# Attention of a two-layer hybrid block on one core: values of three key tiles in one line, newest first, and the last layer's probability sums by products of ones

## Chip, cores and metric

One core of a Trainium2 chip runs the whole program. The metric is the time of one execution on the device in microseconds (us); lower is better. Three executions of the kernel before were timed; a fourth one was taken with the hardware profiler, and every duration below is from that one.

## What is computed

Two layers; each normalises 512 latent and 256 context tokens of width 1024, projects them, runs three token mixers side by side (a recurrent one, a latent attention with 8 heads over all keys, and a grouped attention with 8 heads, a window of 128 and a sink), gates and merges their outputs, and projects back. The change touches the two attentions alone:

```python
def dense_block_attention(q, k, v):
    ...
        s = jnp.einsum('bqhd,bkhd->bhqk', qx, k, preferred_element_type=jnp.float32) * (Dq ** -0.5)
        p = jax.nn.softmax(s, axis=-1).astype(v.dtype)
        return jnp.einsum('bhqk,bkhd->bqhd', p, v)
...
def sink_gqa(q, k, v, sink, valid):
    ...
    s = jnp.where(valid, s, NEG)
    sk = jnp.broadcast_to(sink.astype(jnp.float32).reshape(C_KV_HEADS, C_GROUP, 1, 1), s.shape[:-1] + (1,))
    p = jax.nn.softmax(jnp.concatenate([s, sk], axis=-1), axis=-1)[..., :-1].astype(v.dtype)
    return jnp.einsum('bkgqs,bskd->bqkgd', p, v).reshape(B, Q, H * D)
```

In layer 0 both the 512 latent and the 256 context queries are computed, in the last layer the latent ones alone.

## The kernel before, in words

The program is written as one stream of operations with a scheduler behind it: `band` sets the priority of what is written inside it, the scheduler then puts each engine's instructions in an order by readiness (by its own estimate) and priority, and the chip runs each engine's list in that order. The band `SERVE` (line 84) is ahead of all others. `in_line` (line 148) adds, for each product written inside it, that it comes after the product written before it, in PE's order only; nothing else is forbidden to stand between two of them.

**Attention of one head** (`attend`, lines 1103 and 1314). Keys go in tiles of 128; the queries' 512 latent columns (and in layer 0 apart from them 256 context columns) stand side by side. Per key tile the scores `stp` are two or three products into one of three PSUM banks, which the row maxima `mps` of the next head share. ACT makes the exponentials `pe` from them (`probs`, line 879, the ACT instruction at 882), and POOL adds these up in `acc` (886). `prepare` makes the next head's operands and maxima in between (transposes `trp` or `qtp`, maxima `mps`, `mxp`), and `turns` (833) weaves the two.

**Values.** Each tile's (exponentials, values) goes into the list `late`. `together` (854) takes the oldest three when five or more wait and calls `values` for each (1062 and 1247), which calls `weigh` (932): two float32 products per tile, one for each half of the queries, into `yps` (or `ypc` for the context): the output of one half lies in partitions 0 to 63, that of the other in 64 to 127, 64 output columns of the array each, where scores, maxima and projections use 128. In the trace a float32 product is two MATMULs.

**The end of a head.** `normalise` (889) copies the sums of values (`tb`, 894), forms the sums of probabilities over the partitions of `acc`, and multiplies by their reciprocal (925). With `cols` (the last layer) the sums come as columns: four products of `acc`'s 128 columns with one column of ones, and with the sink's (`er`); a reciprocal of 128x4 (907); and products that spread the columns back over 64 partitions (`rec` times the identity). Without `cols` (layer 0) two products of ones with 256 columns give the sums already spread, the sink comes by eight products of 32 rows, and the reciprocal is 128x256 (924). `gate_out` (783) then loads the gate, multiplies (796) and stores to HBM (792).

**What stands around it.** Filler: the rest of the input projections (`g<-hh`, `g<-hl`), which `pace` and `gates` write in a lower band; in the last layer also the merges of the first two mixers, `early` (1371) and `branch` (1343; `g<-yh`, `g<-yl`). Their operands come from HBM (`ygt`, 1351), are rounded by ACT (`yh`, 1352) with the remainder from POOL (`yl`, 1353), and lie where the input projections' operands (`hh`, `hl`) lay before. `tail` (1382) merges the third mixer, which needs the last head's output, and projects back.

Of the kernel before, what the change touches and what calls it, by code (L numbers as in the profile page):

```python
# [19 lines left out]
P = 128  # L20
# [40 lines left out]
def build(tc, A, out):  # L61
# [737 lines left out]
    def gated(*a):  # L799
        gate_out(*a)  # L800
        yield
# [49 lines left out]
            for _ in x:  # L851
                pass

    def together(late, values, rest=False):

        while len(late) >= (1 if rest else EB - 3):
            for _ in range(min(len(late), 3)):
                values(*late.pop(0))

    def max_tile():  # L860
        return rps.tile([P, 512], F32, tag="r", name="mps", bufs=RB)
# [24 lines left out]
            G.tensor_tensor(acc, keep.pop(0, acc), e, ALU.add)  # L886
        return e

    def normalise(ap, yps, acc, n, y, cols, sink=None):

        h, nt = n // 2, n // P
        tb = ap.tile([P, 256], F32, tag="tb", name="tb", bufs=2)[:, 0:h]
        lo, hi = slice(0, 64), slice(64, 128)
        S.copy(tb, yps)
        yield
        if cols:

            sps = rps.tile([P, 256 + nt], F32, tag="c", name="sps", bufs=CB)
            col, sps = sps[:, 256:256 + nt], sps[:, 0:h]
            for t in range(nt):  # L900
                mm(col[:, t:t + 1], acc[:, t * P:(t + 1) * P], ones[:, 0:1], start=(t == 0), stop=(sink is None),
                   skip_group_check=True)
            if sink:
                er, xr, r0 = sink
                mm(col, er, ident[xr, r0:r0 + nt], start=False, skip_group_check=True)
            rec = ap.tile([P, 4], F32, tag="rec", name="rec", bufs=2)[:, 0:nt]
            V.reciprocal(rec, col)
            for t in range(nt // 2):
                for a, u in ((lo, t), (hi, t + nt // 2)):
                    mm(sps[a, t * P:(t + 1) * P], rec[:, u:u + 1].to_broadcast([P, 64]), ident, start=(t == 0),  # L910
                       skip_group_check=True)
            rec = sps
        else:
            sps = rps.tile([P, 256], F32, tag="c", name="sps", bufs=CB)[:, 0:h]
            for a, c0 in ((lo, 0), (hi, h)):
                mm(sps[a], ones[:, 0:64], acc[:, c0:c0 + h], stop=(sink is None), skip_group_check=True)
            if sink:
                er, xr, r0 = sink
                for t in range(nt // 2):
                    for a, u in ((lo, t), (hi, t + nt // 2)):  # L920
                        mm(sps[a, t * P:(t + 1) * P], ident[xr, r0 + u:r0 + u + 1].to_broadcast([er.shape[0], 64]), er, start=False, stop=(t == nt // 2 - 1),
                           skip_group_check=True)
            rec = ap.tile([P, 256], F32, tag="rec", name="rec", bufs=2)[:, 0:h]
            V.reciprocal(rec, sps)
        V.tensor_tensor(y, tb, rec, ALU.mult)

    def value_sums(n):
        if n == 512:
            return gps.tile([P, 512], F32, tag="m", name="yps", bufs=1)[:, 0:n // 2]
        return rps.tile([P, 512], F32, tag="c", name="ypc", bufs=CB)[:, 0:n // 2]  # L930

    def weigh(o, v, e, c0, first, done):


# [117 lines left out]
    def mla_heads(l, last, ap, qt, kt, vh, scale, tq0, filler):  # L1052
# [8 lines left out]

        def values(hd, k, s0, n, e, acc, y):
            nk = 6 if s0 else 2
            if k == 0:
                sums[hd, s0] = value_sums(n)
            weigh(sums[hd, s0], vh[:, k, hd], e, 0, k == 0, k == nk - 1)
            if k == nk - 1:
                later.append(normalise(ap, sums.pop((hd, s0)), acc[:, s0 - qo:s0 + n - qo], n,
                                       y[:, hd % 2, (s0 - qo) // 2:(s0 + n - qo) // 2], last))
                next(later[-1])  # L1070
                if s0 and hd % 2:
                    later.append(gated(ap, l, 4 + hd // 2, y, segs))
# [30 lines left out]
        def attend(hd):  # L1103
            kh, kl, qh, ql = heads[hd]
            par = hd % 2
            if par == 0:
                ys[hd // 2] = ap.tile([P, 2, (T - qo) // 2], F32, tag="y", name="ymla", bufs=2)
            y = ys[hd // 2]
            acc = ap.tile([P, T - qo], F32, tag="acc", name="acc", bufs=2)
            keep = {}  # L1110
            for s0, n, k in [(s0, n, k) for s0, n in segs[::-1] for k in range(6 if s0 else 2)]:
                ks, sl = slice(k * P, (k + 1) * P), slice(s0 - qo, s0 + n - qo)
                st = rps.tile([P, 512], F32, tag="r", name="stp", bufs=RB)[:, 0:n]
                mm(st, kh[0:xr.stop, ks], qh[0:xr.stop, sl], stop=False)
                mm(st, kl[:, ks], qh[0:96, sl], start=False, stop=False)
                mm(st, kh[0:96, ks], ql[:, sl], start=False)
                late.append((hd, k, s0, n, probs(ap, st, n, scale, acc[:, sl], k, keep, EB), acc, y))
                together(late, values)
                if s0:
                    yield  # L1120
            if hd == 7:
                together(late, values, True)

        turns(8, prepare, attend, later, filler)

# [110 lines left out]
    def gqa_heads(l, F, last, ap, KA, KB, vh, sink8, queries, xs, filler):  # L1236
# [9 lines left out]

        def values(hd, k, g0, s0, e, acc, y):
            kv, nk, n = hd // 4, 6 if g0 else 2, (T if g0 else NC) - g0
            if k == 0:
                sums[hd, g0] = value_sums(n)  # L1250
            weigh(sums[hd, g0], vh[:, k, kv], e, s0 - g0, k == 0, k == nk - 1)
            if k == nk - 1:
                later.append(normalise(ap, sums.pop((hd, g0)), acc[:, g0 - qo:g0 + n - qo], n,
                                       y[:, hd % 2, (g0 - qo) // 2:(g0 + n - qo) // 2], last,
                                       (sinks[hd][xr], xr, xr.start - tq0 + g0 // P)))
                next(later[-1])
                if g0 and hd % 2:
                    later.append(gated(ap, l, 8 + hd // 2, y, segs))

        def prepare(hd):  # L1260

# [52 lines left out]
        def attend(hd):  # L1314
# [7 lines left out]
            for g0, n, k in [(g0, n, k) for g0, n in segs[::-1] for k in range(6 if g0 else 2)]:  # L1322
# [8 lines left out]
                    mm(st[:, o_:o_ + P], win[:, 0], win[:, w], start=False, stop=(e == len(edges) - 1),  # L1331
                       skip_group_check=True)
                late.append((hd, k, g0, s0, probs(ap, st, n, scale, acc[:, s0 - qo:s1 - qo], k, keep, EB), acc, y))
                together(late, values)
                if g0:
                    yield
            if hd == 7:
                together(late, values, True)

        turns(8, prepare, attend, later, filler)  # L1340

# [316 lines left out]
```

## Time and profile before

| what | value |
|---|---|
| median of three runs | 2422.4 us (2420.09 to 2424.84) |
| the profiled execution | 2427.43 us, its span 2425.7 us |
| granted TensorE clock, mean | 0.948 |
| busy: PE, PE's loads, DVE, ACT, POOL | 89%, 68%, 52%, 37%, 36% |
| attention of layer 0 | about 780 to 1160 us of the span |
| attention of the last layer | about 2085 to 2290 us |

PE is TensorE's products, PEld its weight loads, DVE VectorE, ACT ScalarE, POOL GpSimd, SPq the queue that issues DMAs. The end of a PE product is modelled and products overlap, so what one costs in its place is read from the starts of neighbours, not from its length. The granted clock is given as a share of 2.4 GHz.

### The profile page before, as it was taken

Reading aid. Unit: us, or ns where it says so; the run is one execution under the profiler, and the core shown is the slowest. Engines: PE = TensorE matmul, PEld = TensorE weight load, DVE = VectorE, ACT = ScalarE, POOL = GpSimd, SP = SyncE. Lnnn points to the kernel's source line nnn. Section 1 sums busy time; section 2 is a strip of 40 time slices with the busy share of each in tenths; the row PEclk is TensorE's granted clock in tenths of the full one; section 3 lists DMA queues with packets and bytes.
Section 4 is the critical chain, followed back from the end, with each engine's and each line's share of the span. In section 5 each row is a group of like instructions: output and inputs, shape, how many; then the busy total and the mean of one; then the engine's idle time right before and its main releaser. Section 6 shows DMA issues by size and latency. Waiting matters only on the chain. (4 is left out here: it accounts for less than half of the span.)

```text
span 2425.7 us, 42832 instructions
## 1 busy us (share of the span) xinstructions
PE 2148.9 (89%) x16824; PEld 1647.0 (68%) x16824; DVE 1271.8 (52%) x2300; ACT 891.7 (37%) x1654; POOL 870.0 (36%) x699
## 2 busy tenths in 40 slices
PE   7986896887998999899888998799868998999989
PEld 4765674766887667766767786567656876666667
DVE  4475326865338664366135256725668457554423
ACT  3443211233354333543213345332323455434322
POOL 1255211111123344444334224553211144454564
PEclk9988998998999999999989999899978999999999
DMA  7155665555251012511686414566444262102385
GB/s 249 60 144 175 194 197 138 138 132 136 74 170 50 31 44 84 189 33 51 205 256 188 134 57 123 163 206 169 121 113 101 86 209 92 48 18 70 106 261 168
DMA packets 330442, 314.25 MB, mean 130 GB/s; under 512 B 112768, under 2 KB 239488, under 8 KB 330240
## 3 DMA queue, kind: packets, MB, share of 16 engines
q1 hardware_dynamic: 312432, 281.87, 39.5%
q10 hardware_dynamic: 17808, 29.63, 3.9%
q8 instruction: 133, 2.18, 0.4%
q14 instruction: 69, 0.57, 0.1%
HBM read 213.64 MB, written 97.78 MB: 128 GB/s over the span
## 5 line engine op out<-in xcount | busy, mean ns | idle before, releaser
L166 POOL TENSOR_TENSOR wl<-wf,wh 128x512 fp32r<-128x512 f32 x316 | 425.7, 1349 | 1064.0 <-ACT wh L165 977.2
L154 PE MATMUL g<-hh,wh 128*128 128x512 f32 (+1 forms) x1264 | 471.3, 373 | 19.2 <-DVE st L779 10.2
L154 PE MATMUL g<-hh,wl 128*128 128x512 f32 (+1 forms) x1264 | 457.0, 362 | 1.5 <-POOL wl L166 1.4
L154 PE MATMUL g<-hl,wh 128*128 128x512 f32 (+1 forms) x1264 | 456.4, 361 | 0.0
L165 ACT CAST wh<-wf 128x512 fp32r<-128x512 f32 x316 | 195.1, 619 | 500.7 <-PE g L154 249.3
L154 PEld LDWEIGHTS g<-hh,wh 128*128 128x128 f32 x1264 | 249.1, 197 | 71.9 <-issue 15.4
L154 PEld LDWEIGHTS g<-hh,wl 128*128 128x128 f32 x1264 | 249.3, 197 | 41.1 <-issue 7.9
L154 PEld LDWEIGHTS g<-hl,wh 128*128 128x128 f32 x1264 | 249.9, 198 | 40.1 <-issue 11.4
L886 POOL TENSOR_TENSOR acc<-acc,pe 128x512 f32<-128x512 f32 (+2 forms) x128 | 146.2, 1142 | 141.2 <-ACT pe L882 131.7
L882 ACT ACTIVATE pe<-stp 128x256 f32<-128x256 f32 (+2 forms) x224 | 114.4, 522 | 201.1 <-PE stp L154 194.4
L864 DVE TENSOR_REDUCE mx<-mps 128x1 f32<-128x384 f32 (+2 forms) x256 | 127.8, 535 | 69.2 <-PE mps L154 67.0
L154 PE MATMUL yps<-pe,vh 128*64 128x256 f32 (+1 forms) x704 | 133.3, 389 | 0.0
L678 DVE TENSOR_TENSOR YB<-YB,inv 128x30 f32<-128x30 f32 (+9 forms) x180 | 96.4, 536 | 5.3
L154 PE MATMUL g<-yh,wh 128*128 128x512 f32 (+1 forms) x224 | 81.4, 368 | 19.9 <-DVE zt L1368 11.4
L1368 DVE SCALAR_TENSOR_TENSOR zt<-zt,g 128x512 f32<-128x512 f32 (+1 forms) x56 | 31.7, 576 | 117.6 <-PE g L154 85.3
L676 DVE TENSOR_TENSOR inv<-inv,YB 128x30 f32<-128x30 f32 (+9 forms) x180 | 87.3, 485 | 8.5 <-issue 2.3
L777 ACT ACTIVATE st<-g 128x256 f32<-128x256 f32 (+1 forms) x108 | 56.6, 524 | 89.1 <-PE g L154 83.7
L154 PE MATMUL g<-yl,wh 128*128 128x512 f32 (+1 forms) x224 | 83.5, 374 | 6.1 <-POOL yl L1353 6.1
L154 PE MATMUL gc<-hh,wh 128*128 128x512 f32 x192 | 76.7, 400 | 8.6 <-ACT hh L325 4.5
L154 PE MATMUL g<-yh,wl 128*128 128x512 f32 (+1 forms) x224 | 80.4, 363 | 0.0
L154 PE MATMUL scps<-AR,BK 64*128 64x128 f32 (+1 forms) x768 | 65.5, 296 | 14.5 <-DVE TR L644 10.6
L154 PE MATMUL gc<-hl,wh 128*128 128x512 f32 x192 | 78.0, 406 | 0.1
(395 smaller groups left out, 4358.2 us busy)
## 6 DMA issues: line engine op xcount, KB each, us to landing
wf<-w_in SPq DMA_DIRECT2D x163, 256.0 KB, 3.1
wf<-ada_w SPq DMA_DIRECT2D x84, 256.0 KB, 4.0
wf<-w_in ACTq DMA_DIRECT2D x77, 256.0 KB, 3.0
bkd<-bk SPq DMA_DIRECT2D x16, 768.0 KB, 6.3
zt<-thzg SPq DMA_DIRECT2D x48, 256.0 KB, 3.8
wf<-w_bo SPq DMA_DIRECT2D x40, 256.0 KB, 3.5
thzg<-st SPq DMA_DIRECT2D x24, 384.0 KB, 2.4
md<-zt SPq DMA_DIRECT2D x32, 256.0 KB, 3.5
```

Source lines behind the costliest of these rows:

```text
L154: queued(TE.matmul(o, l, r, start=start, stop=stop, **kw))
L165: S.copy(wh, w32)
L166: eng.tensor_tensor(wl, w32, wh.bitcast(F32), ALU.subtract)
L676: V.tensor_tensor(t3, M3[:, 0:j, j:j + 1].to_broadcast([P, j, n]), Y3[:, j:j + 1, j + 1:32].to_broadcast([P, j, n]), ALU.mult)
L678: V.tensor_tensor(Y3[:, 0:j, j + 1:32], Y3[:, 0:j, j + 1:32], t3, ALU.add)
L777: S.activation(t[:, sl], p, AF.Tanh, scale=0.5)
L864: V.tensor_reduce(mx, ps, AX.X, ALU.max)
L882: S.activation(e, st, AF.Exp, scale=scale)
L886: G.tensor_tensor(acc, keep.pop(0, acc), e, ALU.add)
L1368: V.scalar_tensor_tensor(th, th, 1.0, p_, ALU.add, ALU.mult)
```

## The change

`together` takes the same three tiles, but reverses them, so that the newest is written first, and writes their values in the band `SERVE` and in one line. In the grouped attention a tile that covers all queries, or belongs to sums already begun, goes ahead of others (`begins`), since the first product of a sum has to cover all its columns; `values` counts the tiles of a sum in place of asking for the first and last key tile. `normalise` loses its `cols` branch: the last layer now also uses products of ones. The diff, with the calls of `together` left out (each passes `begins`, in the latent attention a function that is always true):

```diff
-    def together(late, values, rest=False):
+    def together(late, values, begins, rest=False):
 
         while len(late) >= (1 if rest else EB - 3):
-            for _ in range(min(len(late), 3)):
-                values(*late.pop(0))
+            some = [late.pop(0) for _ in range(min(len(late), 3))][::-1]
+            with band(SERVE), in_line():
+                for x in sorted(some, key=lambda x: not begins(*x)):
+                    values(*x)
...
-    def normalise(ap, yps, acc, n, y, cols, sink=None):
+    def normalise(ap, yps, acc, n, y, sink=None):
 
         h, nt = n // 2, n // P
         tb = ap.tile([P, 256], F32, tag="tb", name="tb", bufs=2)[:, 0:h]
         lo, hi = slice(0, 64), slice(64, 128)
         S.copy(tb, yps)
         yield
-        if cols:
-
-            sps = rps.tile([P, 256 + nt], F32, tag="c", name="sps", bufs=CB)
-            col, sps = sps[:, 256:256 + nt], sps[:, 0:h]
-            for t in range(nt):
-                mm(col[:, t:t + 1], acc[:, t * P:(t + 1) * P], ones[:, 0:1], start=(t == 0), stop=(sink is None),
-                   skip_group_check=True)
-            if sink:
-                er, xr, r0 = sink
-                mm(col, er, ident[xr, r0:r0 + nt], start=False, skip_group_check=True)
-            rec = ap.tile([P, 4], F32, tag="rec", name="rec", bufs=2)[:, 0:nt]
-            V.reciprocal(rec, col)
-            for t in range(nt // 2):
-                for a, u in ((lo, t), (hi, t + nt // 2)):
-                    mm(sps[a, t * P:(t + 1) * P], rec[:, u:u + 1].to_broadcast([P, 64]), ident, start=(t == 0),
-                       skip_group_check=True)
-            rec = sps
-        else:
-            sps = rps.tile([P, 256], F32, tag="c", name="sps", bufs=CB)[:, 0:h]
-            for a, c0 in ((lo, 0), (hi, h)):
-                mm(sps[a], ones[:, 0:64], acc[:, c0:c0 + h], stop=(sink is None), skip_group_check=True)
...
-            rec = ap.tile([P, 256], F32, tag="rec", name="rec", bufs=2)[:, 0:h]
-            V.reciprocal(rec, sps)
+        sps = rps.tile([P, 256], F32, tag="c", name="sps", bufs=CB)[:, 0:h]
+        for a, c0 in ((lo, 0), (hi, h)):
+            mm(sps[a], ones[:, 0:64], acc[:, c0:c0 + h], stop=(sink is None), skip_group_check=True)
+        if sink:
+            er, xr, r0 = sink
             for t in range(nt // 2):
                 for a, u in ((lo, t), (hi, t + nt // 2)):
-                    mm(sps[a, t * P:(t + 1) * P], rec[:, u:u + 1].to_broadcast([P, 64]), ident, start=(t == 0),
+                    mm(sps[a, t * P:(t + 1) * P], ident[xr, r0 + u:r0 + u + 1].to_broadcast([er.shape[0], 64]), er, start=False, stop=(t == nt // 2 - 1),
                        skip_group_check=True)
...
+        rec = ap.tile([P, 256], F32, tag="rec", name="rec", bufs=2)[:, 0:h]
+        V.reciprocal(rec, sps)
         V.tensor_tensor(y, tb, rec, ALU.mult)
...
         def values(hd, k, g0, s0, e, acc, y):
             kv, nk, n = hd // 4, 6 if g0 else 2, (T if g0 else NC) - g0
-            if k == 0:
-                sums[hd, g0] = value_sums(n)
-            weigh(sums[hd, g0], vh[:, k, kv], e, s0 - g0, k == 0, k == nk - 1)
-            if k == nk - 1:
+            o, i = sums.get((hd, g0)) or (value_sums(n), 0)
+            weigh(o, vh[:, k, kv], e, s0 - g0, i == 0, i == nk - 1)
+            sums[hd, g0] = o, i + 1
+            if i == nk - 1:
...
+        def begins(hd, k, g0, *_):
+            return k < 2 or (hd, g0) in sums
```

What the scheduler makes of it, on PE. First place: the latent attention of the last layer, from one head's last scores into the next head. Before (`64x256` are values or sums of ones, `128x1` the column sums, a row's last number how many follow each other; in this list a float32 product counts once):

```order
L154 MATMUL yps<-pe,vh 64x256 x6
L154 MATMUL mps<-kh_19857,qh_19859 128x384 x3
L154 MATMUL sps<-cst,acc 128x1 x4
L154 MATMUL yps<-pe,vh 64x256
L154 MATMUL mps<-kh_19857,qh_19859 128x384
L154 MATMUL yps<-pe,vh 64x256 x2
L154 MATMUL stp<-qh_19858,kh_19856 128x512
L154 MATMUL stp<-qh_19858,kl 128x512
L154 MATMUL stp<-ql,kh_19856 128x512
L154 MATMUL mps<-kh_19857,qh_19859 128x384 x2
L154 MATMUL sps<-cst,rec 64x128 x3
```

The same place in the changed program:

```order
L154 MATMUL stp<-ql,kh_19857 128x512
L154 MATMUL yps<-pe,vh 64x256 x6
L154 MATMUL mps<-kh_19856,qh_19858 128x384 x3
L154 MATMUL sps<-acc,cst 64x256
L154 MATMUL mps<-kh_19856,qh_19858 128x384
L154 MATMUL sps<-acc,cst 64x256
L154 MATMUL g<-hh,wh 128x512
L154 MATMUL g<-hl,wh 128x512
L154 MATMUL stp<-qh_19859,kh_19857 128x512
L154 MATMUL stp<-qh_19859,kl 128x512
L154 MATMUL stp<-ql,kh_19857 128x512
L154 MATMUL mps<-kh_19856,qh_19858 128x384
```

The next head's first values no longer stand in pieces between maxima and scores; the columns are gone, two products of ones stand for them, and two filler projections have come in.

Second place: the end of the grouped attention in the last layer, the last head's last tile. Before:

```order
L154 MATMUL yps<-pe,vh 64x256
L154 MATMUL yps<-pe,vh 64x128 x2
L154 MATMUL yps<-pe,vh 64x256 x2
L154 MATMUL sps<-cst,acc 128x1 x2
L154 MATMUL g<-yh,wh 128x512
L154 MATMUL sps<-cst,acc 128x1 x2
L154 MATMUL sps<-cst,er 128x4
L154 MATMUL g<-yl,wh 128x512
L154 MATMUL g<-yh,wl 128x512
L154 MATMUL sps<-cst,rec 64x128 x4
```

Now:

```order
L154 MATMUL stp<-win 128x128
L154 MATMUL sps<-acc,cst 64x256
L154 MATMUL g<-yl,wh 128x512
L154 MATMUL yps<-pe,vh 64x256
L154 MATMUL yps<-pe,vh 64x128
L154 MATMUL yps<-pe,vh 64x256 x2
L154 MATMUL yps<-pe,vh 64x128
L154 MATMUL sps<-acc,cst 64x256
L154 MATMUL sps<-er,cst 64x128 x4
L154 MATMUL g<-yh,wl 128x512
```

The merge product here is one of 38 that are left behind the last scores; before, 192 stood behind them, the first of them in the piece above.

## Rows read from the trace of the kernel before

**Rows 1.** The page, part 1: busy time, share of the span, instructions of each engine.

```profile
PE 2148.9 (89%) x16824; PEld 1647.0 (68%) x16824; DVE 1271.8 (52%) x2300; ACT 891.7 (37%) x1654; POOL 870.0 (36%) x699
```

**Rows 2.** Busy time by stretch: length; busy us (count) of PE, PEld, DVE, ACT, POOL; clock; DMA.

```profile
780.00:970.00 190.00, 186.65 (x1054) 130.15 (x1053) 110.50 (x188) 73.13 (x149) 81.20 (x68) 1.00 0.18 53
1035.00:1160.00 125.00, 124.41 (x825) 81.02 (x826) 79.62 (x128) 49.83 (x120) 52.34 (x54) 1.00 0.14 41
2085.00:2195.00 110.00, 109.29 (x611) 70.60 (x611) 53.76 (x109) 42.09 (x81) 56.43 (x43) 1.00 0.11 29
2215.00:2300.00 85.00, 84.93 (x555) 57.77 (x554) 42.48 (x80) 33.26 (x70) 44.42 (x43) 0.98 0.23 69
```

**Rows 3.** PE's waits in 790:970 and 2085:2200, the longest of each: total, times, longest (us).

```profile
PE mxp L154 <- DVE mx L1098: 1.2, 2, 0.7
...
PE sps L154 <- POOL acc L886: 0.7, 1, 0.7
```

**Rows 4.** Timeline of PE, last layer: start us, length, engine, line, operation, count.

```profile
2128.74 0.65 PE L154 MATMUL yps<-pe,vh 128*64 128x256 f32 x2
2129.32 0.50 PE L154 MATMUL stp<-qh,kh 100*128 100x512 f32 x1
2129.66 0.40 PE L154 MATMUL stp<-qh,kl 96*128 96x512 f32 x1
2129.90 0.40 PE L154 MATMUL stp<-ql,kh 96*128 96x512 f32 x1
...
2132.51 0.40 PE L154 MATMUL stp<-ql,kh 96*128 96x512 f32 x1
2132.84 1.52 PE L154 MATMUL yps<-pe,vh 128*64 128x256 f32 x12
2134.29 0.78 PE L154 MATMUL mps<-kh,qh 96*128 96x384 f32 x3
2134.91 0.95 PE L154 MATMUL sps<-cst,acc 128*128 128x1 f32 x8
2135.78 0.43 PE L154 MATMUL yps<-pe,vh 128*64 128x256 f32 x1
...
2273.99 0.65 PE L154 MATMUL yps<-pe,vh 128*64 128x256 f32 x4
2274.57 0.44 PE L154 MATMUL stp<-QA,KA 128*128 128x384 f32 x1
```

**Rows 5.** Timeline, all engines: the end of a head in layer 0.

```profile
1154.68 0.85 PE L154 MATMUL sps<-acc,cst 128*64 128x256 f32 x4
...
1156.05 0.39 PE L154 MATMUL g<-hh,wh 128*128 128x256 f32 x1
...
1156.16 1.76 DVE L924 RECIPROCAL rec<-sps 128x256 f32<-128x256 f32 x1
...
1158.02 0.43 DVE L925 TENSOR_TENSOR ygqa<-tb,rec 128x256 f32<-128x256 f32 x1
```

**Rows 6.** The reciprocal of the last layer: count, duration ns min/median/max, first and last start.

```profile
L907 DVE RECIPROCAL rec<-sps x16: 173/183/183, 2095.6 to 2291.4; 128x4 f32<-128x4 f32 x16
```

**Rows 7.** The last gate; the landing, rounding, remainder of `ygt` and the landing of `ygd`.

```profile
2295.59 1.70 DVE L796 SCALAR_TENSOR_TENSOR gt<-gt,ygqa 128x512 f32<-128x512 f32 x1
...
DMA to landing us min/median/max: 2.5/3.4/5.2
L1352 ACT CAST yh<-ygt x36: 399/613/622, 1183.1 to 2354.0; 128x512 fp32r<-128x512 f32 x24, 128x256 fp32r<-128x256 f32 x12
L1353 POOL TENSOR_TENSOR yl<-ygt,yh x36: 724/1268/1734, 1183.8 to 2354.7; 128x512 fp32r<-128x512 f32 x24, 128x256 fp32r<-128x256 f32 x12
DMA to landing us min/median/max: 1.7/2.6/5.2
```

**Rows 8.** Timeline: a tile's last score product and its exponential.

```profile
2104.49 0.40 PE L154 MATMUL stp<-ql,kh 96*128 96x512 f32 x1
...
2105.06 0.61 ACT L882 ACTIVATE pe<-stp 128x512 f32<-128x512 f32 x1
```

More of the change, by code (lines that the diff above doesn't have):

```diff
@@ L1063, in values @@
             nk = 6 if s0 else 2
-            if k == 0:
-                sums[hd, s0] = value_sums(n)
-            weigh(sums[hd, s0], vh[:, k, hd], e, 0, k == 0, k == nk - 1)
-            if k == nk - 1:
-                later.append(normalise(ap, sums.pop((hd, s0)), acc[:, s0 - qo:s0 + n - qo], n,
-                                       y[:, hd % 2, (s0 - qo) // 2:(s0 + n - qo) // 2], last))
+            o, i = sums.get((hd, s0)) or (value_sums(n), 0)
+            weigh(o, vh[:, k, hd], e, 0, i == 0, i == nk - 1)
+            sums[hd, s0] = o, i + 1
+            if i == nk - 1:
+                later.append(normalise(ap, sums.pop((hd, s0))[0], acc[:, s0 - qo:s0 + n - qo], n,
+                                       y[:, hd % 2, (s0 - qo) // 2:(s0 + n - qo) // 2]))
                 next(later[-1])
@@ L1117, in attend @@
                 late.append((hd, k, s0, n, probs(ap, st, n, scale, acc[:, sl], k, keep, EB), acc, y))
-                together(late, values)
+                together(late, values, lambda *x: True)
                 if s0:
@@ L1121, in attend @@
             if hd == 7:
-                together(late, values, True)
+                together(late, values, lambda *x: True, True)
         turns(8, prepare, attend, later, filler)
@@ L1248, in values @@
             kv, nk, n = hd // 4, 6 if g0 else 2, (T if g0 else NC) - g0
-            if k == 0:
-                sums[hd, g0] = value_sums(n)
-            weigh(sums[hd, g0], vh[:, k, kv], e, s0 - g0, k == 0, k == nk - 1)
-            if k == nk - 1:
-                later.append(normalise(ap, sums.pop((hd, g0)), acc[:, g0 - qo:g0 + n - qo], n,
-                                       y[:, hd % 2, (g0 - qo) // 2:(g0 + n - qo) // 2], last,
+            o, i = sums.get((hd, g0)) or (value_sums(n), 0)
+            weigh(o, vh[:, k, kv], e, s0 - g0, i == 0, i == nk - 1)
+            sums[hd, g0] = o, i + 1
+            if i == nk - 1:
+                later.append(normalise(ap, sums.pop((hd, g0))[0], acc[:, g0 - qo:g0 + n - qo], n,
+                                       y[:, hd % 2, (g0 - qo) // 2:(g0 + n - qo) // 2],
                                        (sinks[hd][xr], xr, xr.start - tq0 + g0 // P)))
@@ L1333, in attend @@
                 late.append((hd, k, g0, s0, probs(ap, st, n, scale, acc[:, s0 - qo:s1 - qo], k, keep, EB), acc, y))
-                together(late, values)
+                together(late, values, begins)
                 if g0:
@@ L1337, in attend @@
             if hd == 7:
-                together(late, values, True)
+                together(late, values, begins, True)
         turns(8, prepare, attend, later, filler)
```

3 lines of the change are left out of this document (removed).

## Prediction

> **What bounds the kernel now.** I read the page's busy shares first: PE is the fullest engine [rows 1]. An average over stages decides nothing, so next the stretches in which the changed lines run: attention of layer 0 (latent attention, then grouped attention) and of the last layer. In all four PE is busy for 98 to 100% of the time at a granted clock of 1.00 (0.98 in the last), the upper of its two levels, 2.4 GHz, while DVE stands at 49 to 64% [rows 2]. Third, what PE waits for there: in the latent attention of either layer the longest entry of its list of waits is 1.2 and 0.7 us [rows 3]. So attention lasts as long as PE's list of products, and what counts is how long that list is in time.
>
> Fourth, the timeline of PE, to see what a product costs in its place [rows 4]. The reader is to take three starts from it. A run of twelve value products (three key tiles, two halves of the queries, two passes each in the trace, since these products are float32) lasts from 2132.84 to the next wide product at 2134.29: 1.45 us. A run of four (one tile) lasts 0.58 us. A run of two, which is one half of one tile, lasts 0.58 us as well. Two halves that stand side by side run at the same time; one half alone takes as long as both. Hence 0.435 us for a tile, (1.45 - 0.58)/2, and 0.145 us of each run for going back to wide products. Going in costs too: the twelve start 0.33 us after the score product before them, where score products follow each other by 0.24 (2129.66, 2129.90), so 0.10. **A run costs 0.245 us beside its work.**
>
> Now the count. I walked through PE's order of both programs and cut it at each change between the 64-column products (values, sums of ones) and the others; a half that stands alone counts as a whole pass. (Before, the values of 224 tiles stand in 172 pieces and 81 tiles are torn; now in 73 pieces, no tile torn. Some sums of ones stand next to them, others alone.)
>
> | | runs | 0.435 us passes | 128-column passes |
> |---|---|---|---|
> | layer 0, before / now | 111 / 73 | 124 / 104 | 70 / 62 |
> | last layer, before / now | 84 / 52 | 99 / 109 | 49 / 8 |
>
> A 128-column pass streams half as much; I estimate half of 0.435, 0.22 us.
>
> **The change, part by part.** *Layer 0*: only the line moves. 38 runs x 0.245 = 9.3; 20 passes x 0.435 = 8.7; 8 x 0.22 = 1.8; inside the runs there are 6 fewer turns to the sink's 32-row products, at a run's price 1.5. Sum 21.3 us less on PE. All other products of the layer are the same.
>
> *Last layer, values*: 32 runs x 0.245 = 7.8 less. *Sums*: the 16 column blocks go. One is eight products of one column, 0.87 us from 2134.91 to 2135.78 [rows 4]; 16 x 0.87 = 13.9 less, and the sink's two in each of 8 heads, at an eighth of a block each, 1.7 less. The broadcasts go (32 of the 41 passes that disappear): 41 x 0.22 = 9.0 less. In their place come two products of ones per head, one pass: the 99 passes become 109, 16 more for sums and 6 fewer for values, 10 x 0.435 = 4.4 more. The sink's eight small products per head in grouped attention: in layer 0 four sums and eight sink products last 1.37 us together (1154.68 to 1156.05) [rows 5]; less 0.145 and 0.435 that leaves 0.79, so 8 x 0.79 = 6.3 more. Sum 21.7 us less.
>
> The removed columns are where the Trainium skill speaks otherwise. The Trainium skill's page "TensorE: Matmul & The Clock Gate", section "Back-to-back issue gap", gives a product of 1 to 64 columns some 60 cycles, 25 ns; by that a block of eight would be an estimated 0.2 us, and the whole sum about 11 us smaller. The row's 0.87 decides; the smaller sum, 2396, gets no chance of its own.
>
> *On DVE* a reciprocal of 4 columns, 0.18, becomes one of 256 columns, 1.76 us, and the multiplication behind it stays at 0.4 [rows 5, 6]: 16 x 1.58 = 25 us more on DVE. What hides it is PE's own list; in layer 0 the same reciprocals stand beside a DVE at 58 to 64% and PE does not wait [rows 2, 3]. In the last layer DVE would come from 49 to 56% to about 65 to 70%. A row maximum that stands behind a reciprocal holds one of three PSUM banks that scores and maxima share, so some may show: bounds 0 and 25; I take 4, near to what layer 0 shows.
>
> *Filler moves.* The scheduler takes more filler products into attention: 753 instead of 634 in layer 0, and in the last layer 154 merge products beside the 89 input projections that stood there already. That moves work and adds none. But the merge's operands reuse the space of the projections' operands, so a load (3.4 us to landing), the rounding (0.61) and the remainder on POOL (1.27) stand between the last projection and the first merge product [rows 7]: 5.3 us. In the order about 4.3 us of attention lies between them. I take 2 us, bounds 0 and 6.
>
> *The end of attention.* Before, 192 merge products stood behind the last score product; now 38. Behind the last head's sums come reciprocal 1.76, product 0.42, gate 1.70, store 2.6, load 3.4, rounding 0.61 [rows 5, 7]: 10.5 us before the tail's fourth operand is there. In the order 36 merge products and 27 tail products that need only the first three operands follow, as wide as the score products that stand 0.24 us apart [rows 4]: 15 us. Covered by 4 us, so nothing; up to 8 if the gate waits behind other DVE work.
>
> DMAs are as many as before, in other places of SP's queue; ACT, DVE and POOL issue as many instructions.
>
> **Sum.** 21.3 + 21.7 = 43 us less, plus 4 and 2 back: 37 us. The profiled execution took 2427.4 us (span 2425.7); the median of the three runs is 2422.4, 0.2% below. Taken from the median: **2385 us**.
>
> **Rivals.**
> *The line makes PE wait.* Each group now begins with its newest tile, and everything behind it on PE, scores of the next tiles too, stands until that exponential is done. A tile's last score product starts at 2104.49, its exponential ends at 2105.67 [rows 8]: 1.18 us. If the group stood right behind that tile, PE would lose some 0.95 us. There are 76 groups (64 tiles by 3 in each attention of layer 0, 48 by 3 in the last layer), so from 43/76 = 0.57 us a group the gain is gone, and at 0.95 us the kernel is 72 - 37 = 35 us slower, 2457. For it: PE takes its list in order, the waits of [rows 3] are waits of the whole engine. The Trainium skill says so too, on the page named above, section "The mechanism": products start and end strictly in program order. Against it: by the columns at 2.4 GHz, 206 of the 224 tiles have over 1.2 us of other products between their scores and their values in the new order, and what the other 18 lack adds up to under 4 us. Chance 0.06: half of it slower, half nothing.
>
> *The last layer runs out of cover.* DVE's 25 us show in full, or the end of attention and the first merge lose 8 + 6 us: with DVE 2385 + 21 = 2406, with all of it some 2418; a part of this gives 2395 to 2408. For it: these stretches are where the scheduler's idea of a reciprocal's length matters. Against it: layer 0. Chance 0.25, still faster by over 0.2% nearly throughout.
>
> *Layer 0 gains nothing.* Its filler ends earlier, but if something other than PE sets the time up to the last layer, the 21.3 us are lost there: 43 - 21 - 6 = 16 us remain, 2406. Against it: the filler that follows is the same kind of products. Chance 0.05. (That the line does not close up is no rival: the order shows whole groups.)
>
> **How the numbers follow.** Forecast 0.64; cover 0.25; layer 0 0.05; waits 0.06. Below: nothing given back, and the prices of a run and a pass, read beside other neighbours than some will have, 15% short: 49 us, near 2372. Above: 2408 leaves out the worst of the second rival and the first. A measurement of this kernel tells about 0.2%, 5 us, from no change. Faster 0.91; same 0.05; slower 0.04.
>
> **What would show it.** Runs of twelve value products of 1.45 us; no 128x1 products; reciprocals x48 near 1.3 us mean; the last layer's attention longer by its 154 fillers (37 us at 0.24) less 22, and what follows shorter. Wrong, if PE's waits in attention name ACT's exponential or DVE's maxima with over 15 us, or if the end of attention shows a gap of over 5 us before the tail.

## The result and the profile after

The changed kernel took 2387.8 us (median of four runs, 2385.2 to 2390.4) against 2423.6 for the kernel before: a ratio of **0.985, interval 0.983 to 0.987**, 36 us less. A second comparison (experiment 9) gave 0.9853 (0.9835 to 0.9871). The forecast was 2385 us, 37 us less.

Profile after, the page's first part; it answers to [rows 1]:

```profile
PE 2104.1 (88%) x16680; PEld 1624.5 (68%) x16680; DVE 1303.6 (55%) x2300; ACT 891.0 (37%) x1654; POOL 867.3 (36%) x699
```

PE has 45 us less to do and the span is 38 us shorter; DVE has 32 us more.

Where in the program? The table of windows, cut at events that both programs have: attention of layer 0 from its first to its last score product, from there to the recurrent mixer of the last layer, that mixer up to the next first score product, attention of the last layer, from its last score product to the first product of the tail, the tail. Columns as in [rows 2]. The kernel before:

```profile
797.50:1152.40 354.90, 342.68 (x2046) 237.40 (x2045) 198.76 (x344) 148.06 (x323) 155.23 (x142) 1.00 0.23 71
1152.40:1637.40 485.00, 426.40 (x2525) 345.37 (x2523) 217.28 (x317) 167.10 (x287) 197.92 (x155) 0.94 0.55 167
1637.40:2076.90 439.50, 375.53 (x4014) 300.45 (x4013) 269.04 (x529) 174.66 (x322) 130.70 (x103) 0.91 0.46 127
2076.90:2288.40 211.50, 210.72 (x1251) 137.73 (x1250) 109.01 (x215) 88.02 (x174) 110.13 (x93) 0.99 0.16 46
2288.40:2346.90 58.50, 50.68 (x223) 38.91 (x221) 13.36 (x20) 12.29 (x22) 31.88 (x27) 0.96 0.75 239
2346.90:2425.60 78.70, 71.16 (x288) 54.54 (x288) 26.80 (x32) 19.84 (x33) 38.26 (x28) 0.96 0.58 189
```

The changed kernel:

```profile
799.50:1160.90 361.40, 344.19 (x2166) 251.26 (x2164) 199.41 (x344) 152.91 (x333) 161.41 (x147) 1.00 0.25 76
1160.90:1621.70 460.80, 403.23 (x2405) 325.91 (x2404) 217.37 (x316) 162.73 (x279) 191.12 (x151) 0.94 0.55 171
1621.70:2059.90 438.20, 372.03 (x4014) 298.10 (x4013) 268.73 (x529) 174.00 (x321) 130.03 (x103) 0.92 0.46 128
2059.90:2291.10 231.20, 223.02 (x1268) 148.44 (x1267) 148.60 (x227) 97.45 (x190) 136.61 (x113) 1.00 0.32 98
2291.10:2304.70 13.60, 12.21 (x64) 8.83 (x62) 6.53 (x8) 3.85 (x8) 9.82 (x9) 1.00 0.38 122
2304.70:2387.50 82.80, 73.24 (x288) 56.54 (x288) 27.14 (x33) 18.45 (x31) 33.90 (x26) 0.93 0.52 172
```

Read in pairs of rows, since filler moved from the second row of a pair into the first. Layer 0 (rows one and two) went from 839.9 to 822.2, 17.7 us less; the mixer between is the same program and took 1.3 less; the last layer (rows four to six) from 348.7 to 327.6, 21.1 less. Both attentions became longer by themselves, by 6.5 and 19.7 us, because more filler runs in them; the 58.5 us between the last scores and the tail became 13.6. DVE stands at 64% in the last layer's attention (148.60 of 231.20), and PE no longer at 100% but at 96%.

PE's waits in the last layer's attention (2062 to 2300 us of the changed kernel; engine, tile, line, releaser, then total, times, longest):

```profile
PE g L154 <- POOL yl L1341: 3.9, 3, 1.9
PE stp L154 <- DVE QA L878: 1.1, 2, 0.9
PE sps L154 <- POOL acc L889: 1.0, 2, 0.6
PE mxp L154 <- DVE mx L1295: 0.7, 1, 0.7
PE stp L154 <- DVE qh L878: 0.7, 1, 0.7
PE stp L154 <- ACT pe L885: 0.7, 3, 0.3
PE mxp L154 <- DVE mx L1083: 0.3, 1, 0.3
```

Before, the list of that stretch had the one entry of [rows 3], 0.7 us. What came in is merge products that wait for the remainder of their operand (3.9 in three waits, of which the first merge's is 1.9) and products that wait for DVE (2.8 together). On the other side stand the waits around the merges behind the last scores. Before (2288 to 2350; the tail's first product is the `gc` that waits 3.3 us, at 2346.92, so that the 0.8 lies in the tail):

```profile
PE gc L154 <- ACT yh L1352: 3.3, 1, 3.3
PE g L154 <- POOL yl L1353: 2.4, 4, 1.3
PE g L154 <- ACT yh L1352: 1.7, 1, 1.7
PE gc L154 <- POOL yl L1353: 0.8, 1, 0.8
```

Changed, on PE's timeline from the tail's first product on (in brackets the idle time before a row, and what ended it):

```profile
2304.66 0.73 PE L154 MATMUL gc<-yh,wh 128*128 128x512 f32 x2 [1.00 <-ACT yh L1340]
...
2308.05 0.79 PE L154 MATMUL gc<-yl,wh 128*128 128x512 f32 x1 [2.42 <-POOL yl L1341]
...
2317.62 0.49 PE L154 MATMUL gc<-yh,wh 128*128 128x512 f32 x1 [1.66 <-ACT yh L1340]
2318.96 0.80 PE L154 MATMUL gc<-yl,wh 128*128 128x512 f32 x1 [0.85 <-POOL yl L1341]
```

So 1.0 us of waits for an operand stands before the tail, and the others came into it: the tail takes 82.8 us, where it took 78.7.

The timeline of PE in the changed kernel, the same place as [rows 4] (a head's first values, then the sums of the head before), and the end of a head of the grouped attention:

```profile
2119.96 1.51 PE L154 MATMUL yps<-pe,vh 128*64 128x256 f32 x12
2121.40 0.79 PE L154 MATMUL mps<-kh,qh 96*128 96x384 f32 x3
2122.13 0.65 PE L154 MATMUL sps<-acc,cst 128*64 128x256 f32 x2
2122.70 0.44 PE L154 MATMUL mps<-kh,qh 96*128 96x384 f32 x1
...
2286.94 0.65 PE L154 MATMUL sps<-acc,cst 128*64 128x256 f32 x4
2287.52 0.65 PE L154 MATMUL sps<-er,cst 4*64 4x128 f32 x8
2288.11 0.44 PE L154 MATMUL stp<-QA,KA 128*128 128x384 f32 x1
```

The run of twelve lasts 1.44 us as forecast (2119.96 to 2121.40). The two products of ones stand apart here, 0.57 us each (2122.13 to 2122.70), where side by side they last 0.58 together (2286.94 to 2287.52). The sink's eight last 0.59 behind them.

**A balance that all experiments use.** In each trace I added up three things, from the first scores of layer 0 on and without the mixer between the layers. The *list* is what the prediction had priced: every run of 64-column products from its start to the start of the next other product, with 0.10 us for going in, and the columns in the same way. PE's idle time inside it is left out, and what ran at the lower of the clock's two levels (1.2 and 2.4 GHz) counts half. *Waits* are PE's idle times over 0.1 us. *Clock* is half of the time that the granted clock spent at the lower level, an estimate of what that cost. Before, the list is 108.1 us in layer 0 and 91.4 in the last, the waits 70.3 and 12.4, the clock 29.0 and 7.4. Differences from before, in us, each as layer 0 / last layer; the measured one is the ratio's, on some 2428:

| kernel | measured (interval) | list | waits | clock |
|---|---|---|---|---|
| changed | -36 (-42 to -31) | -21.4 / -23.8 | +4.1 / +2.9 | +1.7 / -1.8 |
| 9 changed again | -36 (-40 to -31) | -21.4 / -23.8 | +2.3 / +2.7 | -1.7 / -1.7 |
| 1 line, layer 0 only | -11 (-15 to -6) | -21.4 / +0.3 | +2.1 / +0.9 | +1.7 / -1.9 |
| 2 line, columns kept | -16 (-20 to -11) | -21.4 / -12.3 | +4.2 / +6.7 | +6.8 / +1.1 |
| 3 sums by ones only | -6 (-9 to -2) | 0 / -13.5 | -3.1 / +6.8 | +1.7 / -1.9 |
| 4 halves apart | -18 (-25 to -11) | -9.0 / -15.9 | -2.7 / +0.8 | +5.1 / -0.6 |
| 5 groups of one | +4 (0 to +9) | -3.6 / -14.9 | -1.8 / +11.8 | +3.4 / +9.9 |
| 6 right behind | -30 (-37 to -23) | -20.5 / -23.4 | +5.0 / +9.1 | -5.1 / +3.3 |
| 7 band, no line | -27 (-33 to -20) | -17.8 / -21.8 | -1.7 / +11.6 | -3.4 / +1.6 |
| 8 oldest first | -42 (-50 to -35) | -20.2 / -24.2 | -1.0 / +4.4 | +1.7 / -0.3 |
| 10 sums in line too | -43 (-48 to -37) | -27.1 / -26.4 | +2.9 / +2.8 | +8.5 / +0.3 |
| 11 groups of six | -69 (-74 to -64) | -28.9 / -29.4 | -5.9 / +2.4 | -5.1 / -4.0 |
| 12 six and sums | -26 (-31 to -21) | -31.2 / -34.7 | -0.8 / +19.4 | +6.8 / +13.1 |

The three together give the change of a layer's length in its trace to within 4 us (5 in layer 0 of kernel 7). A single profile carries some 8 us of its own besides: the same program ahead of the first attention ends between 797.5 and 805.4 us in these traces. So a difference of a few us in this table says nothing.

### The profile page after: what moved, and what is told of

The parts are those of the page before. It is cut to its first block, busy times and chain, and to the rows that moved or that the text cites. A ratio compares the mean times of both kernels' runs of the same rounds, so it can differ in the third digit from the quotient of the medians.

```text
span 2387.5 us, 42421 instructions
## 1 busy us (share of the span) xinstructions
PE 2104.1 (88%) x16680; PEld 1624.5 (68%) x16680; DVE 1303.6 (55%) x2300; ACT 891.0 (37%) x1654; POOL 867.3 (36%) x699
## 5 line engine op out<-in xcount | busy, mean ns | idle before, releaser
L154 PE MATMUL yps<-pe,vh 128*64 128x256 f32 (+1 forms) x704 | 94.8, 379 | 0.1
L678 DVE TENSOR_TENSOR YB<-YB,inv 128x30 f32<-128x30 f32 (+9 forms) x180 | 90.4, 502 | 5.3
L909 DVE RECIPROCAL rec<-sps 128x256 f32<-128x256 f32 (+1 forms) x48 | 70.3, 1478 | 33.6 <-PE sps L154 33.4
L889 POOL TENSOR_TENSOR acc<-pe 128x512 f32<-128x512 f32 (+1 forms) x48 | 53.7, 1118 | 83.0 <-ACT pe L885 73.9
L642 DVE TENSOR_TENSOR AR<-scps,cst 64x256 f32<-64x256 f32 x96 | 40.1, 418 | 72.0 <-PE scps L154 70.9
```

The costliest lines, as they stand in the source:

```text
L642: V.tensor_tensor(AR[oth, pds, 2 * par, :], ps[oth, :, a0:a0 + 64], msk("ms", oth), ALU.mult)
L678: V.tensor_tensor(Y3[:, 0:j, j + 1:32], Y3[:, 0:j, j + 1:32], t3, ALU.add)
```

## Experiments

### 1 to 3: which part makes the gain

Three kernels take the change apart. 1 has the line in layer 0 only (`together` asks `not last`), the last layer is as before. 2 has the line in both layers, and `normalise` with `cols`:

```diff
-    def normalise(ap, yps, acc, n, y, sink=None):
+    def normalise(ap, yps, acc, n, y, cols, sink=None):
...
```

3 has products of ones in the last layer, but takes values as before:

```diff
-            some = [late.pop(0) for _ in range(min(len(late), 3))][::-1]
-            with band(SERVE), in_line():
-                for x in sorted(some, key=lambda x: not begins(*x)):
-                    values(*x)
+            for _ in range(min(len(late), 3)):
+                values(*late.pop(0))
```

> Values in one line in layer 0; the last layer is written as in the kernel before (three tiles oldest first, no line, sums as columns). Theory (prices of runs and torn passes): PE's list loses what the prediction puts on layer 0, 21 us, so about 2402 us against 2424 before (2398 to 2407), and the last layer's first score product stands some 20 us earlier, the rest of the trace as before. Rival (layer 0's gain is lost in the stages between the two attentions, the last layer made it all): 2418 to 2424 us.

> Values in one line in both layers, but the last layer keeps its sums as columns and the short reciprocals. Theory: by the terms of the prediction the last layer's values give 10 us and its sums 11, so without the sums' part and without the 4 us of DVE that were given back this stands some 7 us above the changed kernel, about 2395 us; a recount of this kernel's own order (fewer lone passes than those terms had) says 2387. So 2385 to 2398. Rival (in the last layer the removed columns are the gain, the line gives nothing there): about 2402 us. Second rival (the long reciprocals cost more than the columns did): under 2383 us.

> Only the other half of the change: products of ones in the last layer, values taken oldest first and in no line in both layers. Theory: the sums' terms are 11 us less on PE and 4 back on DVE, 2417 us; a recount of this kernel's order, in which more products of ones stand alone, makes it 6 less and 4 back, 2422. So 2414 to 2424. Rival (the columns' removal is the larger part of the whole gain): 2395 to 2408 us.

Measured: 0.9956 (0.9938 to 0.9974), 0.9936 (0.9916 to 0.9956) and 0.9976 (0.9962 to 0.9991): 11, 16 and 6 us less. 1 and 2 missed: 21 and about 30 had been expected. 3 came out within its range: the terms of the prediction made it 7 us less, the recount of its order 2.

The list did what it should, or more. In the last layer alone the line takes off 12.3 us (10.4 forecast) and the sums 13.5 (11.3 forecast). But of that the last layer's own time, first scores to the end, shrank by 3.7 us in kernel 2 and 5.5 in kernel 3, and with both by 21. The sum of two halves is 9.2; the whole is 21. Most of the difference stands in the column of waits: 6.7 and 6.8 us came back in either half, 2.9 in the whole. PE's waits between the last scores and the tail in kernel 2 (2299 to 2342):

```profile
PE gc L154 <- ACT yh L1358: 5.0, 1, 5.0
```

and in kernel 3 (2296 to 2342):

```profile
PE gc L154 <- ACT yh L1338: 3.4, 1, 3.4
```

They are the longest of that stretch, as in the kernel before. With 105 and 128 merge products left behind the last scores (192 before, 38 in the changed kernel), PE's idle time up to the tail stays, 8 us in all three; and in attention, where the other merges went, new waits of 5 us came in, in kernel 2 the first merge product's for `yh` with 3.8, in kernel 3 products that wait for DVE. Of these four, only the changed kernel has so little left that the old waits go (1.4 us there).

In layer 0, kernel 1 has the changed kernel's list to 0.1 us. In its trace the layer is 14.2 us shorter, in the changed kernel's two traces 17.6 and 17.4; by the runs it is 11, at most 15. So layer 0's list is as forecast, and 4 to 7 us of it come back in the traces, more by the runs. Waits are 2 to 4 us of that; where the rest goes these traces do not settle.

### 4: both halves of a tile apart

```diff
-                mm(o[rows, a - i * h:b - i * h], v, e[:, a - c0:b - c0], start=first, stop=done, skip_group_check=True)
+                go = lambda rows=rows, a=a, b=b, i=i: mm(o[rows, a - i * h:b - i * h], v, e[:, a - c0:b - c0], start=first, stop=done, skip_group_check=True)
+                go() if i == 0 else second.append(go)
...
```

`second` is emptied at the end of a line and of a sum.

> The changed kernel, but inside each line of three tiles all first halves of the queries stand ahead of all second halves, so that few products have their other half beside them: the same products, the same number of runs. Theory (a half alone costs as much as both): about 100 more whole passes of 0.435 us and 25 of half the columns at 0.22, some 44 us more than the changed kernel, about 2432 us; a run of twelve in the latent attention lasts 2.3 instead of 1.45 us. Rival (what counts is how many products there are and how often PE goes into and out of them): 2388 us, runs of twelve still at 1.45.

Measured: 0.9925 (0.9895 to 0.9955), 18 us more than the changed kernel, between the two. The run of twelve with all first halves ahead:

```profile
2129.69 2.00 PE L154 MATMUL yps<-pe,vh 128*64 128x256 f32 x12
2131.62 0.38 PE L154 MATMUL mxp<-cst,mx 128*4 128x128 f32 x2
```

1.93 us, where halves side by side take 1.45. So pairs do run at the same time, and a torn tile costs; but a half costs a full 0.435 only where it ends a run. In this run, where halves stand behind their like, one costs 0.30 on average: (1.93 - 0.145)/6. The list, 20 us longer than the changed kernel's (12.4 and 7.9), accounts for the 18 measured.

### 5: groups of one

```diff
-            some = [late.pop(0) for _ in range(min(len(late), 3))][::-1]
+            some = [late.pop(0) for _ in range(min(len(late), 1))][::-1]
```

> The changed kernel, but a group takes one tile instead of three as soon as five wait. The runs so far allow the runs of 64-column products to be added up by their measured lengths: 200 us before, 156 in the changed kernel. In this kernel's order there are 237 such runs instead of 125, with the tiles still whole: 178.5 us. Theory (a run costs beside its work): 23 us more than the changed kernel, less up to 5 us of waits for exponentials, so 18 to 23 us more, 0.9925 to 0.9945 of the kernel before. Rival (whole tiles and early values are the gain, the length of a run does not matter): as the changed kernel, 0.985.

Measured: 1.0018 (1.0001 to 1.0036), 41 us more than the changed kernel: the rival is out, and the theory has half of it. The list is 27 us longer, where 23 had been counted. The other part stands in the last layer: 9 us more of waits, and a clock that was lower for longer (12 us by the estimate of the balance). In its attention (2080 to 2348) PE ran dry:

```profile
PE g L154 <- ACT yh L1340: 5.4, 3, 3.8
PE stp L154 <- DVE mx L867: 3.0, 2, 2.6
...
PE mps L154 <- DVE mx L867: 2.1, 1, 2.1
```

This is the prediction's second rival (the last layer runs out of cover) at work: row maxima, and merges that came before their operands were there.

### 6 and 7: does the line make PE wait for exponentials?

6 takes a group as soon as three tiles wait, 7 drops the line:

```diff
-        while len(late) >= (1 if rest else EB - 3):
+        while len(late) >= (1 if rest else EB - 5):
```

```diff
-            with band(SERVE), in_line():
+            with band(SERVE):
```

> The changed kernel, but a group of three is taken as soon as three tiles wait instead of five, so that its newest tile's exponential stands close before it. By the widths of the products in between at 2.4 GHz, 82 tiles (15 in the changed kernel) have under 1.18 us of other products between their last score product and their values, and lack 24 us together (5 there); the runs themselves are 3 us shorter. Theory (PE takes its list in order and stands until the exponential is done): 16 us more than the changed kernel, 0.990 to 0.993 of the kernel before, and PE's waits in attention name ACT's exponential with some 20 us. Rival (what is missing is hidden elsewhere, for instance because attention already waits for something else): within 4 us of the changed kernel, 0.985.

> The changed kernel with the values in the band ahead of all others, newest first, but without the line. Its order has 140 runs instead of 125, 4 us more by their measured lengths, and 90 tiles lack 31 us of cover (15 and 5 in the changed kernel). Theory: 4 + 25 us more than the changed kernel, 0.995 to 0.998 of the kernel before, nearly all of it PE's waits for ACT's exponential. Rival (the band alone makes the gain and the line adds nothing): within 5 us of the changed kernel, 0.985 to 0.987.

Measured: 0.9876 (0.9848 to 0.9905) and 0.9890 (0.9863 to 0.9916), 6 and 10 us more than the changed kernel by the ratios, where 16 and 29 were expected. Both intervals overlap that of the changed kernel (0.983 to 0.987), so that neither is shown to be slower. Exponentials are not what costs. They are waited for, but by the weight loads of the values. Last layer's attention (2060 to 2292) of kernel 6:

```profile
PEld yps L154 <- ACT pe L885: 7.6, 23, 0.6
```

of kernel 7:

```profile
PEld yps L154 <- ACT pe L885: 9.3, 31, 0.4
```

and of the changed kernel:

```profile
PEld yps L154 <- ACT pe L885: 0.7, 2, 0.4
```

0.3 us each, and most of that passes while the product before still runs: on PE itself the entry for values and exponentials is 0.3 us in kernel 6 and absent in 7. My estimate had put the whole of 1.18 us against the widths of the products between. If these kernels lose something, their traces show it elsewhere: 85 and 90 merge products stay behind the last scores, and the first merge product in attention waits for its operand, 5.0 us in kernel 6 and 5.2 in kernel 7, of which this is the row (2062 to 2300):

```profile
PE g L154 <- ACT yh L1340: 5.2, 1, 5.2
```

So the band alone makes most of the gain: without the line the list is only 5.6 us longer, too little to be told from the waits here. What the line adds these runs do not show.

### 8: oldest first

```diff
-            some = [late.pop(0) for _ in range(min(len(late), 3))][::-1]
+            some = [late.pop(0) for _ in range(min(len(late), 3))]
```

> The changed kernel with the three tiles in line oldest first. Its order has 122 runs instead of 125, 1 us less by their measured lengths, and 6 tiles lack 1.4 us of cover instead of 15 and 5. Theory (the line does it, which tile begins is of no account, since an exponential is nearly always done): within 5 us of the changed kernel, 0.983 to 0.987. Rival (the newest has to begin, else PE waits in the middle of a run for the tile that comes last): 10 us or more slower than the changed kernel, 0.989 or above.

Measured: 0.9826 (0.9796 to 0.9856), the interval overlaps that of the changed kernel. That the newest tile goes first is no part of the gain.

### 9 to 12: a longer run

10 puts the products of ones and the sink's into the band and each behind the one before it; 11 takes six tiles when seven wait, the older head's ahead; 12 has both:

```diff
+        with band(SERVE):
+            mm(sps[lo], ones[:, 0:64], acc[:, 0:h], stop=(sink is None), skip_group_check=True)
+            with in_line():
+                mm(sps[hi], ones[:, 0:64], acc[:, h:2 * h], stop=(sink is None), skip_group_check=True)
...
```

```diff
-        while len(late) >= (1 if rest else EB - 3):
-            some = [late.pop(0) for _ in range(min(len(late), 3))][::-1]
+        while len(late) >= (1 if rest else EB - 1):
+            some = [late.pop(0) for _ in range(min(len(late), 6))][::-1]
             with band(SERVE), in_line():
-                for x in sorted(some, key=lambda x: not begins(*x)):
+                for x in sorted(some, key=lambda x: (x[0], not begins(*x))):
```

> The changed kernel once more, beside the three that follow, so that they can be compared with it on one chip. 0.983 to 0.987 of the kernel before.

> The changed kernel, with the products of ones of a head (and the sink's) also in the band ahead of all others, each behind the one before it in line, so that the two halves stand side by side. Its order has 98 runs of 64-column products instead of 125; by the measured lengths of such runs (unknown ones by the prices) 10 us less on PE. Theory (the list's length is the time): 5 to 10 us less than the changed kernel, 0.981 to 0.983 of the kernel before. Rival (sums that go ahead of other work make PE wait for the POOL's last sum of exponentials, and fewer merge products are left behind the last scores): as the changed kernel or up to 10 us more.

> The changed kernel, but a group takes six tiles as soon as seven wait (of eight buffers). Its order has 95 runs instead of 125, 16 us less by their lengths, and lacks less cover for exponentials. Theory (the list's length is the time): 10 to 16 us less than the changed kernel, 0.978 to 0.981 of the kernel before. Rival (with seven of eight buffers full the exponentials wait for a buffer, scores for the exponentials' banks; no merge product is left behind the last scores, so that the end of attention stands bare, 5 to 18 us as in the groups of one): 0.983 to 0.990.

> Both edits together: groups of six and the sums in line. 79 runs instead of 125, 23 us less by their lengths. Theory: 13 to 23 us less than the changed kernel, 0.975 to 0.980 of the kernel before. Rival as for the groups of six, the end of attention stands bare: 0.981 to 0.988.

Measured on one chip: 9 2391.95 us, 10 2384.0 (0.9824, 0.9801 to 0.9848), 11 **2358.75 (0.9716, 0.9697 to 0.9735)**, 12 2402.1 (0.9892, 0.9871 to 0.9913).

10 is 8 us under the changed kernel by the medians, but the intervals overlap. 11 beats both kernels, 33 us below the changed one, over twice what the list explains (13 less than in kernel 9). By the balance another 8 us are waits, and 6 the clock: in all four runs of kernel 11 the mean granted clock is 0.948 to 0.951, in those of kernel 9 0.944 to 0.947. The waits that went stand behind layer 0's attention. The changed kernel again (1165 to 1314) has

```profile
PE g L154 <- ACT yh L1340: 6.6, 4, 5.0
```

the first merge products waiting for their operand, and kernel 11 in the same stretch (1156 to 1290)

```profile
PE g L154 <- ACT yh L1340: 0.5, 2, 0.3
```

Its waits in layer 0 are 8 us fewer than in kernel 9. That this order happens to bring the operand in time is what the trace shows; that longer groups cause it was not tested (kernel 8, with groups of three, has 0.3 us there as well).

12 has the shortest list of all and is 43 us slower than 11. PE's waits in its last attention (2051 to 2315):

```profile
PE sps L154 <- POOL acc L889: 7.5, 4, 3.8
PE g L154 <- ACT yh L1342: 5.7, 3, 3.7
PE stp L154 <- DVE QA L878: 2.6, 2, 1.7
```

Sums that go ahead of everything wait for POOL's last addition, and all of PE's list with them. With groups of six, that is: kernel 10 has the same sums ahead, waits 3.5 us for POOL in that stretch (2062 to 2300), and is not slower than the changed kernel. The 7.5 us are also only the longest of some 25 us of waits there, and another 13 us of the last layer are the clock's.

## Why the prediction was right

**PE's list bounds attention: held.** Layer 0: forecast 21.3 us, measured on the list 21.4. Last layer: 21.7, measured 23.8. Together 43 against 45. The prices of a run and of a pair held to 0.01 us (1.44 and 0.57 to 0.58 in the timeline after). Two terms of the last layer were mis-sized: the columns took 17.5 us by their starts in the trace before, where 15.6 had been counted; and the sink's eight products last 0.59 us behind four sums (2287.52 to 2288.11), not 0.79, so that they cost 1.6 us less over eight heads. The row of [rows 5] that gave the 0.79 holds four sums that did not all run side by side: the sink's first product there starts at 1155.46, 0.78 us after theirs. That a half costs a full pass was too simple (experiment 4), but erred little, as layer 0's list shows.

**DVE, 4 us given back: about right.** The products that wait for DVE in the last attention add up to 2.8 us. DVE's 32 us more on the page are the 25 of the reciprocals, which last as in [rows 5], and 6 of the last layer's multiplication behind them, which was taken to stay at 0.4. Of the last attention:

```profile
L909 DVE RECIPROCAL rec<-sps 128x256 f32<-128x256 f32 x15 | 26.3, 1756 | 15.6 <-PE sps L154 15.5
L910 DVE TENSOR_TENSOR ymla<-tb,rec 128x256 f32<-128x256 f32 x8 | 7.7, 965 | 0.1
```

Before, these eight multiplications, with the reciprocals in PSUM, took 0.41 to 0.42 us each; now, with `rec` in SBUF, they take 0.97 on average. That the mean of all 48 reciprocals would be near 1.3 us was wrong: it is 1.48 on the page.

**First merge product, 2 us between 0 and 6: 1.9** (its remainder `yl`). Two later waits for `yl`, 1.3 and 0.7 us, were not in the forecast; they make up the 3.9 of the entry above.

**End of attention, nothing: right by its sum, wrong in its parts.** The path to the tail's fourth operand was to take 10.5 us and to be covered; it took 22.5, from the last reciprocal (2295.08) to the rounded operand (2317.57), and the cover fell short by 2.5 us (1.66 and 0.85 in the rows above). The prediction let the store follow the gate at once. The gate and its last store in the changed kernel:

```profile
2297.75 1.67 DVE L796 SCALAR_TENSOR_TENSOR gt<-gt,ygqa 128x512 f32<-128x512 f32 x1
...
2311.06 0.59 SPq L792 DMA_DIRECT2D ygd<-gt  x1
```

11.6 us lie between them, in which SP's queue issues DMAs of the merges and of the weights. Another 2.4 us are waited for the first operand's remainder. On the other side the stretch behind the last scores had 7.8 us of idle time before, which the prediction did not count: "following shorter" was put down as moved work alone. In all, PE's idle time in attention rose by 7.5 us, up to the tail it fell by 6.4, and in the tail it rose by 1.8. This cancelling is also why the prediction's terms could be added: in experiments 2 and 3 either half of the change by itself returned 8 to 9 us of its list's gain in the last layer, and a sum of terms for such a half would have been that much too low.

**Layer 0:** the forecast passed all of its 21 us on to what follows. By the traces of the changed kernel 17.5 arrived. That 37 was forecast and 36 measured is so in part luck: layer 0 passed on 4 us less than was forecast, and the last layer shrank by 21 us, where its terms with 6 given back make 16.

**The rivals.** The line does not make PE wait (experiments 6 to 8): its 0.95 us a group does not exist even where tiles stand close. The last layer without cover is real: its waits are 12 and 19 us above those of the kernel before in kernels 5 and 12, beside 3 in the changed kernel. Layer 0 gaining nothing: no, 11 us by the runs (experiment 1).

**The columns.** The 0.87 us of a block decided against the rule of the Trainium skill's page "TensorE: Matmul & The Clock Gate", section "Back-to-back issue gap". That table is for the isolated product; the section itself says that it under-counts at small widths where weights are loaded in between. The trace before agrees with the row: 144 products of the column blocks and the sink, 17.5 us, 0.12 each, not 0.025, and a load for each product [rows 1].

## What to carry to other kernels

Where PE is full, price its list by places: from the start of a group of narrow products to the start of the next wide one. Going in and out cost 0.245 us here, and two halves of the array cost as one only while they stand side by side, so that longer runs may pay again: six tiles in a row beat three by 33 us, of which the list explains 13. Then ask of each wait around the stretch whether it stays: filler that moves into a full stretch brings its operands' waits along, and whether the old ones go depends on how much of it is left behind. Work that others finish late (sums of POOL's additions) can hold up everything in the front band, as in kernel 12.

## What the hardware showed that was not expected

Halves of 64 columns behind their like cost 0.30 us on average, not 0.435 (1.93 against 1.45 us for the twelve). And where PE waited in attention its clock often fell as well: in kernel 12 PE is busy for 90% of the last attention, and its granted clock there is 0.94, a mean between its two levels (2.4 and 1.2 GHz), where the changed kernel has 1.00 at 96%:

```profile
2051.20:2314.50 263.30, 237.69 (x1296) 160.55 (x1295) 147.94 (x231) 101.56 (x196) 146.50 (x120) 0.94 0.32 99
```

It stood at the lower level for 34 us there, in six falls, each shortly after waits of PE. But waits are not all that goes before a fall. In the kernel before, PE was busy throughout when the clock fell at 2284.6 (the 0.98 of [rows 2]), and that row shows the price:

```profile
2285.35 2.80 PE L154 MATMUL yps<-pe,vh 128*64 128x256 f32 x10
2288.08 0.39 PE L154 MATMUL stp<-QA,KA 128*128 128x256 f32 x1
```

These ten products last 2.73 us at the lower level; in the changed kernel the same ten last 1.44 (2289.31 to 2290.75). By the balance's estimate the clock took 13 us of kernel 12's last layer and 10 of kernel 5's. Their other runs agree: the mean granted clock is 0.936 to 0.939 in kernel 12 and 0.938 to 0.943 in kernel 5, where the kernel before has 0.942 to 0.949 beside them. No expectation had counted it.
